# A transformer step on one core: the first feed-forward product of 20 of 22 gate/up pairs in seven block products instead of eight

## The chip, the cores and the metric

The kernel runs on one core of a Trainium2 chip. The metric is device microseconds (us) of one execution. Five engines matter here: PE (TensorE, the matrix unit), DVE (VectorE), ACT (ScalarE), POOL (GpSimd), and SP, which here only issues transfers. Each engine takes its instructions from a queue of its own in a fixed order; an instruction that waits for another engine holds everything behind it in that queue.

## What is computed

One layer of a hybrid network on 640 tokens (128 context, 512 latent) of width 1024, all float32: a token-mixing part, then a feed-forward part (2816 hidden channels). The change touches the feed-forward part:

```python
x = x + gt1 * rms_norm(y, norm_gains[1])
h = rms_norm(x, norm_gains[2]) * (1 + sc2) + sh2
gate, up = jnp.split(h @ w_ffn_in, 2, axis=-1)
y = (jax.nn.silu(gate) * up) @ w_ffn_out
x = x + gt2 * rms_norm(y, norm_gains[3])
```

## The kernel before

Float32 accuracy on PE comes from splits: an operand is kept as a high part (a cast to fp32r) and a low part (the rest), and every product is three matmuls, high by high, high by low, low by high (`mm3`, L81; its matmuls are lines L83, L84, L85). A split of a weight tile is done in halves of 512 columns: ACT casts the high part (L57), DVE subtracts for the low part (L58). Weight tiles come by SP transfers of 512 KB (`wr`), and their split parts `wh`, `wl` live in two pools of two slots each. The pools give a slot out again when the last reader of the tile in it is done.

The order in which each engine takes its instructions is set when the program is built. Around the output projection and the first feed-forward pairs PE's order is written out by hand (the loop under `manual_schedule`); elsewhere a scheduler places instructions by priority and by when it expects their inputs. `high()` raises the priority.

The end of the program goes through these stages:

- merge of two branches, into `mh`, `ml` (high and low part of the merged activations, 8 tiles of 128 channels by 640 tokens); beside it the sums for a gate row `gt1` (matmuls L208, L209 of `cph`, `cpl`, multiplied by `grow` in L225);
- output projection `acc<-woh,mh`, norm and modulation, token tile by token tile. `modulate` writes the next sub-layer's input back into `mh`, `ml` (L1083, L1084);
- first feed-forward product, `ffn(j, s)`: pair j is the gate tile and the up tile (128 hidden channels each), 8 tiles of k, three matmuls each, for a slice of the tokens. ACT takes silu of the gate (L1100), DVE multiplies by up (L1101), ACT and DVE split the result into `ah[j]`, `al[j]` (L1102, L1103). Pairs 0 and 1 run in slices of 384 and 256 tokens, in the hand-written order; pairs 2 to 21 in two halves of 320 tokens, so 2 x 2 x 8 x 3 = 96 matmuls of 320 columns per pair;
- second feed-forward product, `part`: two passes of 512 output channels, each with 11 steps `kk` of two k tiles, for five token tiles: 30 matmuls of 512 columns per step. In the first pass a generator (`row_job`) also sums the rows of a modulation block on DVE (L196);
- last norm, residual, output.

SBUF space is a stack of pools: a new pool lies where a closed one lay, and its tiles wait for the last users of the tiles that they cover. `fp0` holds `ah`, `al` of pairs 0 to 2; on it lies `bp2`, which holds the split weights of the output projection (`woh`, `wol`) and the norm's tiles.

## Time and profile before

| what | value |
|---|---|
| median of three runs | 1106.92 us (1103.74 to 1113.27) |
| profiled execution, span from first to last instruction | 1107.7 us |
| PE busy | 1054.9 us, 95% |
| DVE, ACT, POOL busy | 700.2, 416.4, 139.3 us |

The profiled execution has no time of its own besides its span; the span lies 0.8 us above the median. A busy PE counts overlapping matmuls: a matmul of 320 columns is listed with 0.31 us, but the next one starts 0.147 us after it, so PE's real price is read from starts and not from durations.

### The profile page before, as it was taken

What the parts mean: (1) busy time and instruction counts of PE and PEld (TensorE: products, weight loads), DVE (VectorE), ACT (ScalarE), POOL (GpSimd) and SP (SyncE); (2) the same over time, 40 slices, a digit from 0 to 9 for tenths busy, and PEclk for the clock granted to TensorE, in tenths of its full rate; (3) what the DMA queues carried; (4) which work ended last, traced back from release to release, by engine and by line L of the source; (5) the groups of instructions that cost most, each with busy time, mean ns of one, the idle gap of its engine ahead of it and who ended that gap; (6) DMA issues with size and microseconds to landing.
All of it is one profiled execution on the core that took longest, in us unless ns stands there. A gap on an engine that the chain in (4) does not pass through costs nothing.

```text
span 1107.7 us, 19821 instructions
## 1 busy us (share of the span) xinstructions
PE 1054.9 (95%) x7993; PEld 964.1 (87%) x7993; DVE 700.2 (63%) x1470; ACT 416.4 (38%) x809; POOL 139.3 (13%) x168
## 2 busy tenths in 40 slices
PE   6999988989889989999999999999999999999997
PEld 2699888779788888899998899999999999888885
DVE  5868996997888887986986853333333333464226
ACT  5668436428415333434235552222222222123110
POOL 2225411242242230101000000000000000000000
PEclk9999989998979999999999999999999999999998
DMA  9335621182164266548825412222222222452214
GB/s 345 135 90 155 177 70 64 58 190 83 53 147 124 75 140 235 170 146 304 302 94 179 168 44 91 76 77 76 77 76 77 77 77 77 152 190 76 95 39 152
DMA packets 46822, 139.43 MB, mean 126 GB/s; under 512 B 9453, under 2 KB 9970, under 8 KB 46730
## 3 DMA queue, kind: packets, MB, share of 16 engines
q1 hardware_dynamic: 42170, 125.01, 33.2%
q0 software_dynamic: 4560, 13.15, 5.4%
q8 instruction: 63, 1.03, 0.4%
q14 instruction: 29, 0.24, 0.1%
HBM read 115.47 MB, written 12.18 MB: 115 GB/s over the span
## 4 chain that ended last, share of the span: by engine, by line
PE 74%; DVE 11%; DMA 1%; ACT 1%; issue 1%; SPq 0%; DVEq 0%; POOL 0%; ACTq 0%
PE d L84 16%; PE d L85 16%; PE d L83 16%; PE acc L84 6%; PE acc L85 6%; PE acc L83 6%; DVE otmp L556 2%; PE s L640 2%; DVE X L558 2%; DVE wl L58 2%; PE v L611 1%; PE v L670 1%; DVE RT L562 1%; DMA AQ<-ea 1%; PE w L528 1%
## 5 line engine op out<-in xcount | busy, mean ns | idle before, releaser
L57 ACT CAST wh<-wr 128x512 fp32r<-128x512 f32 x238 | 138.1, 618 | 282.5 <-PE d L84 166.6
L58 DVE TENSOR_TENSOR wl<-wr,wh 128x512 fp32r<-128x512 f32 x238 | 162.0, 711 | 122.3 <-ACT wh L57 121.8
L84 PE MATMUL d<-hT,wh 128*128 128x320 f32 x720 | 230.0, 320 | 0.0
L83 PE MATMUL d<-hT,wh 128*128 128x320 f32 x720 | 228.5, 318 | 1.2 <-DVE cy L721 1.2
L85 PE MATMUL d<-hT,wl 128*128 128x320 f32 x720 | 228.9, 318 | 0.4 <-DVE wl L58 0.4
L83 PE MATMUL d<-mh,wh 128*128 128x320 f32 (+2 forms) x704 | 217.2, 309 | 0.0
L84 PE MATMUL d<-ml,wh 128*128 128x320 f32 (+2 forms) x704 | 217.1, 308 | 0.0
L85 PE MATMUL d<-mh,wl 128*128 128x320 f32 (+2 forms) x704 | 217.1, 308 | 0.0
L83 PEld LDWEIGHTS d<-hT,wh 128*128 128x128 f32 x720 | 138.2, 192 | 4.0 <-DVE cy L721 1.7
L85 PEld LDWEIGHTS d<-hT,wl 128*128 128x128 f32 x720 | 138.4, 192 | 3.3 <-issue 0.7
L84 PEld LDWEIGHTS d<-hT,wh 128*128 128x128 f32 x720 | 138.4, 192 | 2.9 <-issue 0.3
L83 PEld LDWEIGHTS d<-mh,wh 128*128 128x128 f32 x704 | 132.0, 187 | 0.1
L84 PEld LDWEIGHTS d<-ml,wh 128*128 128x128 f32 x704 | 132.0, 188 | 0.0
L85 PEld LDWEIGHTS d<-mh,wl 128*128 128x128 f32 x704 | 132.0, 187 | 0.0
L1101 DVE TENSOR_TENSOR zf<-zf,d 128x320 f32<-128x320 f32 x40 | 19.6, 489 | 131.7 <-PE d L85 131.7
L196 DVE SCALAR_TENSOR_TENSOR gacc<-wr,cv,gacc 128x1024 f32<-128x1024 f32 x64 | 80.1, 1278 | 18.1 <-DMA wr<-in_w_mod_dram 13.7
L83 PE MATMUL acc<-wh,ah 128*128 128x512 f32 x220 | 85.6, 389 | 0.0
L84 PE MATMUL acc<-wl,ah 128*128 128x512 f32 x220 | 85.6, 389 | 0.0
L85 PE MATMUL acc<-wh,al 128*128 128x512 f32 x220 | 85.6, 389 | 0.0
L190 POOL MEMSET gacc<- 128x1024 f32 x8 | 7.5, 963 | 365.5 <-PE d L85 305.7
L85 PEld LDWEIGHTS acc<-wh,al 128*128 128x128 f32 x220 | 41.3, 188 | 8.7
L83 PEld LDWEIGHTS acc<-wh,ah 128*128 128x128 f32 x220 | 41.3, 188 | 8.5
(302 smaller groups left out, 1581.0 us busy)
## 6 DMA issues: line engine op xcount, KB each, us to landing
wr<-in_w_in_dram SPq DMA_DIRECT2D x45, 512.0 KB, 3.3
wr<-in_w_ffn_in_dram SPq DMA_DIRECT2D x44, 512.0 KB, 3.3
wr<-in_w_mod_dram SPq DMA_DIRECT2D x32, 512.0 KB, 3.7
wr<-in_w_ffn_out_dram SPq DMA_DIRECT2D x22, 512.0 KB, 3.2
mr<-in_w_mod_dram SPq DMA_DIRECT2D x16, 512.0 KB, 8.4
thd<-gt SPq DMA_DIRECT2D x16, 320.0 KB, 3.0
bth<-thd SPq DMA_DIRECT2D x16, 320.0 KB, 4.0
wr<-in_w_br_dram SPq DMA_DIRECT2D x8, 512.0 KB, 6.8
```

What stands on the lines that cost most here:

```text
L57: (high or nc.scalar.copy)(out=hi[:, s], in_=raw[:, s])
L58: (low or nc.vector).tensor_tensor(out=lo[:, s], in0=raw[:, s], in1=hi[:, s].bitcast(F32), op=ALU.subtract)
L83: mm(out, lhsT=ah, rhs=bh, start=start, stop=False)
L84: mm(out, lhsT=ah, rhs=bl, start=False, stop=False)
L85: mm(out, lhsT=al, rhs=bh, start=False, stop=stop)
L196: nc.vector.scalar_tensor_tensor(out=acc[v], in0=w, scalar=self.cv[:, k, v:v + 1], in1=acc[v], op0=ALU.mult, op1=ALU.add)
L528: mm(pw[c2 * 64:c2 * 64 + 64, t * P:(t + 1) * P], lhsT=kq3[hs, 0, n, :], rhs=kq3[hs, :, n, :], start=True, stop=True)
L556: nc.vector.tensor_tensor(out=t, in0=B[:, j + 1:32, j:j + 1].broadcast_to([P, n, j]), in1=X[:, j:j + 1, 0:j].broadcast_to([P, n, j]), op=A ...
L558: nc.vector.tensor_tensor(out=X[:, j + 1:32, 0:j], in0=X[:, j + 1:32, 0:j], in1=t, op=ALU.subtract)
L562: nc.vector.transpose(out=RT.rearrange("p m x -> p x m"), in_=X)
L640: mm(ps[half(c2), o:o + 64], lhsT=w(d, c2, t, hd), rhs=R[:, d, c2, t, hd, :], start=True, stop=True)
L1101: nc.vector.tensor_tensor(out=a, in0=a, in1=pu, op=ALU.mult)
```

## The change

- Pairs 2 to 21 (`K1`, `K2` are the two halves of the eight k tiles, `ta`, `tb` the two halves of the tokens). Gate and up weights are a 2 x 2 block matrix, gate K1 (A11), gate K2 (A12), up K1, up K2 (A22); the activations are B11, B12 (K1 of ta, tb), B21, B22. Seven block products of 4 k tiles by three matmuls of 320 columns (`block`) take the place of eight. For that `prepare(j)` forms S1 to S4 of the raw weights (four additions or subtractions of 512 columns on DVE) and splits seven blocks; `combos` forms T1 to T4 of the activations once (DVE and ACT instructions of 1280 columns); T3 is written over B12, in `mh`, `ml`.
- A pair's products run in `first` (2 blocks), `second` (3) and `third` (2). PE's order is written out: first(j), third(j-1), second(j). Accumulators A and C are copied out by ACT in the middle (`p1`, `u2`, `u3`) and accumulated on.
- The result is kept whole, as `act[j]`. The split into high and low part is done later, in `split_act`, beside the second product; 12 split tiles of each kind fit, so pass 2 goes through the steps backwards, uses the last six steps' splits again and makes ten tiles' splits a second time.
- `fp0` holds two tiles (`act0`, `act1`) instead of six.
- Comments and docstrings are emptied, which moves line numbers.

The core of the diff:

```diff
-        ah = [fp0.tile([P, TOK], F32R, name=f"ah{j}") for j in range(3)]
-        al = [fp0.tile([P, TOK], F32R, name=f"al{j}") for j in range(3)]
+        act = [fp0.tile([P, TOK], F32, name=f"act{j}") for j in range(2)]
...
                 return
             pg, pu = half_done[j], self.gemm_cm(wf_in[j][1], h2, s)
-            a = fa()[:, 0:s.stop - s.start]
-            nc.scalar.activation(out=a, in_=pg, func=AF.Silu)
-            nc.vector.tensor_tensor(out=a, in0=a, in1=pu, op=ALU.mult)
-            nc.scalar.copy(out=ah[j][:, s], in_=a)
-            nc.vector.tensor_tensor(out=al[j][:, s], in0=a, in1=ah[j][:, s].bitcast(F32), op=ALU.subtract)
+            nc.scalar.activation(out=act[j][:, s], in_=pg, func=AF.Silu)
+            nc.vector.tensor_tensor(out=act[j][:, s], in0=act[j][:, s], in1=pu, op=ALU.mult)
...
-        # feed-forward network
-        fz, turn = zp.tile([P, 4, TOK], F32, name="zf"), itertools.cycle(range(4))
-        fa = lambda: fz[:, next(turn)]
         fst, fp = stack("fp")
+        txst, tx = stack("tx", side="right")
+        wgst, wg = stack("wg")
         past, psa = stack("psa2", 5, space=PSUM)
-        for j in range(3, FT):
-            ah.append(fp.tile([P, TOK], F32R, name=f"ah{j}"))
-            al.append(fp.tile([P, TOK], F32R, name=f"al{j}"))
         for j in range(2, FT):
-            for h in range(2):
-                ffn(j, slice(h * HALF, (h + 1) * HALF))
+            act.append(fp.tile([P, TOK], F32, name=f"act{j}"))
+        ta, tb = slice(0, HALF), slice(HALF, TOK)
+        K1, K2 = slice(0, 4), slice(4, 8)
+        B12, B22 = (mh[:, K1, tb], ml[:, K1, tb]), (mh[:, K2, tb], ml[:, K2, tb])
+        B11, B21 = (mh[:, K1, ta], ml[:, K1, ta]), (mh[:, K2, ta], ml[:, K2, ta])
+        T1, T2, T4 = ([tx.tile([P, 4, HALF], F32R, name=f"T{n}{x}") for x in "hl"] for n in (1, 2, 4))
+        T3 = B12
+        prepared, weights = {}, itertools.cycle((self.wpool, wf))
+        def load_j(j):
+            pl = (self.rpool, wg)[j % 2]
...
+        def prepare(j):
+            g, u = load_j(j)
+            slots = []
+            for _ in range(4):
+                pl = next(weights)
+                slots.append([pl.tile([P, KT, P], F32R, name="w" + x, tag="w" + x) for x in "hl"])
+            part = lambda x, n: [t[:, 4 * n:4 * n + 4] for t in slots[x]]
+            S = [wg.tile([P, 4, P], F32, name="S", tag="S", bufs=4) for _ in range(4)]
+            def halves(dst, src):
+                nc.scalar.copy(out=dst[0], in_=src)
+                nc.vector.tensor_tensor(out=dst[1], in0=src, in1=dst[0].bitcast(F32), op=ALU.subtract)
+                return dst
+            tt = lambda o, a, b, op: nc.vector.tensor_tensor(out=o, in0=a, in1=b, op=op)
+            o = {}
+            o["A11"] = halves(part(0, 0), g[:, K1])
+            tt(S[0], u[:, K1], u[:, K2], ALU.add)
+            o["S1"] = halves(part(0, 1), S[0])
+            tt(S[1], S[0], g[:, K1], ALU.subtract)
+            o["S2"] = halves(part(1, 0), S[1])
+            o["A12"] = halves(part(1, 1), g[:, K2])
+            tt(S[2], g[:, K1], u[:, K1], ALU.subtract)
+            o["S3"] = halves(part(2, 0), S[2])
+            o["A22"] = halves(part(3, 0), u[:, K2])
+            tt(S[3], g[:, K2], S[1], ALU.subtract)
+            o["S4"] = halves(part(3, 1), S[3])
+            prepared[j] = o
+        def combos():
+            tt = lambda o, a, b, op: nc.vector.tensor_tensor(out=o, in0=a, in1=b, op=op)
+            zz = zp.tile([P, 2, 4, HALF], F32, name="zf")
+            t1, t2, t3 = zz[:, 0], zz[:, 1], wg.tile([P, 4, HALF], F32, name="t3")
...
+            whole(t1, B11)
+            whole(t2, B12)
+            tt(t1, t2, t1, ALU.subtract)
+            halves(T1, t1)
+            whole(t3, B22)
+            tt(t1, t3, t1, ALU.subtract)
+            halves(T2, t1)
+            tt(t2, t3, t2, ALU.subtract)
+            halves(T3, t2)
+            whole(t3, B21)
+            tt(t3, t3, t1, ALU.subtract)
+            halves(T4, t3)
+        def block(ps, A, B, start, stop):
+            for k in range(4):
+                for n, (x, y) in enumerate(((0, 0), (0, 1), (1, 0))):
+                    nc.tensor.matmul(ps, lhsT=A[x][:, k], rhs=B[y][:, k], start=start and k == 0 and n == 0,
+                                     stop=stop and k == 3 and n == 2, skip_group_check=True)
+        acc = lambda: psa.tile([P, 512], F32, name="acc", tag="acc")[:, 0:HALF]
+        tmp = lambda n: wg.tile([P, HALF], F32, name=n, tag=n)
+        add = lambda o, a, b: nc.vector.tensor_tensor(out=o, in0=a, in1=b, op=ALU.add)
+        def first(j):
+            o = prepared[j]
+            A, C = acc(), acc()
+            block(A, o["A11"], B11, True, True)
+            p1 = tmp("p1")
+            with high():
+                nc.scalar.copy(out=p1, in_=A)
+            block(C, o["S1"], T1, True, True)
+            return dict(o=o, A=A, C=C, p1=p1)
+        def second(j, v):
+            o, A, C = v["o"], v["A"], v["C"]
+            block(A, o["S2"], T2, False, True)
+            u2, u3 = tmp("u2"), tmp("u3")
+            with high():
+                nc.scalar.copy(out=u2, in_=A)
+            B = fd()[:, 0:HALF]
+            block(B, o["A12"], B21, True, True)
+            with high():
+                add(act[j][:, ta], v["p1"], B)
+                nc.scalar.activation(out=act[j][:, ta], in_=act[j][:, ta], func=AF.Silu)
+            block(A, o["S3"], T3, False, True)
+            with high():
+                nc.scalar.copy(out=u3, in_=A)
+                add(act[j][:, tb], u3, C)
+            v["u2"] = u2
+        def third(j, v):
+            o, A, C = v["o"], v["A"], v["C"]
+            block(A, o["A22"], T4, False, True)
+            with high():
+                nc.vector.tensor_tensor(out=act[j][:, ta], in0=act[j][:, ta], in1=A, op=ALU.mult)
+            block(C, o["S4"], B22, False, True)
+            with high():
+                g = tmp("gb")
+                add(g, v["u2"], C)
+                nc.scalar.activation(out=g, in_=g, func=AF.Silu)
+                nc.vector.tensor_tensor(out=act[j][:, tb], in0=act[j][:, tb], in1=g, op=ALU.mult)
+        prepare(2)
+        with high():
+            combos()
+        with tc.manual_schedule(engines={mybir.EngineType.PE}):
+            last = None
+            for j in range(2, FT):
+                if j + 1 < FT:
+                    prepare(j + 1)
+                v = first(j)
+                if last:
+                    third(j - 1, last)
+                second(j, v)
+                last = v
+            third(FT - 1, last)
+        wgst.close()
+        txst.close()
         mst.close()
...
             return self.split(raw, [P, 2, 512], "w", next(pools))
-        def part(acc, w, kk, t):
...
+        def split_act(kk):
+            for k in (2 * kk, 2 * kk + 1):
+                hi, lo = (sp.tile([P, TOK], F32R, name="a" + x, tag="a" + x, bufs=12) for x in "hl")
+                nc.scalar.copy(out=hi, in_=act[k])
+                nc.vector.tensor_tensor(out=lo, in0=act[k], in1=hi.bitcast(F32), op=ALU.subtract)
+                parts_of[k] = hi, lo
+        def part(acc, w, kk, t, order):
             s = slice(t * P, (t + 1) * P)
             for i in range(2):
                 k = 2 * kk + i
-                self.mm3(acc, ah[k][:, s], al[k][:, s], w[0][:, i], w[1][:, i], k == 0, k == FT - 1)
+                self.mm3(acc, parts_of[k][0][:, s], parts_of[k][1][:, s], w[0][:, i], w[1][:, i],
+                         kk == order[0] and i == 0, kk == order[-1] and i == 1)
         TAIL = 4
         NK = FT // 2
         acc = [psa.tile([P, 512], F32, name="acc", tag="acc") for _ in range(NT)]
-        for kk in range(NK):
+        order = list(range(NK))
+        for kk in order:
+            split_act(kk)
             w = load_f(I["w_ffn_out"][0, kk])
             for t in range(NT):
-                part(acc[t], w, kk, t)
+                part(acc[t], w, kk, t, order)
             if kk >= 2:
                 next(fill, None)
...
             nc.vector.tensor_tensor(out=y0[:, t, :], in0=gt2[:, min(t, 1), 0:512], in1=acc[t], op=ALU.mult)
         acc = [psa.tile([P, 512], F32, name="acc", tag="acc") for _ in range(NT)]
-        for kk in range(NK - TAIL):
+        order = order[::-1]
+        for kk in order[:-TAIL]:
+            if kk < NK - 6:
+                split_act(kk)
             w = load_f(I["w_ffn_out"][1, kk])
             for t in range(NT):
-                part(acc[t], w, kk, t)
-        ws = [load_f(I["w_ffn_out"][1, kk]) for kk in range(NK - TAIL, NK)]
+                part(acc[t], w, kk, t, order)
+        ws = []
+        for kk in order[-TAIL:]:
+            split_act(kk)
+            ws.append(load_f(I["w_ffn_out"][1, kk]))
         for t in range(NT):
-            for i, w in enumerate(ws):
-                part(acc[t], w, NK - TAIL + i, t)
+            for kk, w in zip(order[-TAIL:], ws):
+                part(acc[t], w, kk, t, order)
             with tc.high_priority(offset=100000):
                 xx = fq.tile([P, D], F32, name="fx", tag="fx", bufs=2)
```

Three places where the order of instructions changes. DVE at the end of the merge (`wol` is the low part of the output projection's weights; the number behind a name is a buffer's). Before:

```order
L225 TENSOR_TENSOR gt1_5970<-grow_5973,d_6598 128x512 [waits PE_49]
L988 TENSOR_TENSOR bth_6530<-bth_6528,bth_6530 128x640 [waits DVE_49]
L58 TENSOR_TENSOR wol_6648<-wr_6645,woh_6647 128x512 [waits Activation_49]
L58 TENSOR_TENSOR wol_6656<-wr_6653,woh_6655 128x512 [waits Activation_49]
L990 TENSOR_TENSOR ml_5976<-bth_6530,mh_5975 128x640 [waits Activation_49]
L58 TENSOR_TENSOR wol_6648<-wr_6645,woh_6647 128x512
L58 TENSOR_TENSOR wol_6656<-wr_6653,woh_6655 128x512
L225 TENSOR_TENSOR gt1_5970<-grow_5973,d_6602 128x512 [waits PE_49]
L58 TENSOR_TENSOR cpl_6607<-gacc_5972,cph_6606 128x512 [waits Activation_49] x2
L225 TENSOR_TENSOR gt1_5970<-grow_5973,d_6612 128x512 [waits PE_49]
L225 TENSOR_TENSOR gt1_5970<-grow_5973,d_6616 128x512 [waits PE_49]
L58 TENSOR_TENSOR wol_6664<-wr_6661,woh_6663 128x512 [waits DMAHW2_49,Activation_49]
```

and with the change:

```order
L225 TENSOR_TENSOR gt1_5970<-grow_5973,d_6598 128x512 [waits PE_49]
L988 TENSOR_TENSOR bth_6530<-bth_6528,bth_6530 128x640 [waits DVE_49]
L225 TENSOR_TENSOR gt1_5970<-grow_5973,d_6602 128x512 [waits PE_49]
L58 TENSOR_TENSOR cpl_6607<-gacc_5972,cph_6606 128x512 [waits Activation_49]
L990 TENSOR_TENSOR ml_5976<-bth_6530,mh_5975 128x640 [waits Activation_49]
L58 TENSOR_TENSOR cpl_6607<-gacc_5972,cph_6606 128x512
L225 TENSOR_TENSOR gt1_5970<-grow_5973,d_6612 128x512 [waits PE_49]
L225 TENSOR_TENSOR gt1_5970<-grow_5973,d_6616 128x512 [waits PE_49]
L58 TENSOR_TENSOR wol_6644<-wr_6641,woh_6643 128x512 [waits Activation_49]
L58 TENSOR_TENSOR wol_6652<-wr_6649,woh_6651 128x512 [waits Activation_49]
L58 TENSOR_TENSOR wol_6644<-wr_6641,woh_6643 128x512 [waits Activation_49]
L58 TENSOR_TENSOR wol_6652<-wr_6649,woh_6651 128x512 [waits Activation_49]
```

The first four subtractions for `wol` stood on both sides of the last merged tile (`ml`); now they stand behind all of the gate row's work (`cpl`, `gt1`).

DVE at the start of pair 2, from the end of `modulate` of the last token tile on. Before:

```order
L1083 CAST mh_5975<-hf_7351 128x4x128 [waits Activation_49]
L1084 TENSOR_TENSOR ml_5976<-hf_7351,mh_5975 128x4x128 [waits DVE_49]
L1101 TENSOR_TENSOR fa_7399<-fa_7399,d_7374 128x384 [waits PE_49]
L1103 TENSOR_TENSOR al1_6636<-fa_7399,ah1_6633 128x384 [waits Activation_49]
L58 TENSOR_TENSOR wl_7566<-wr_7563,wh_7565 128x512 [waits DMAHW4_49,PE_49,Activation_49]
L58 TENSOR_TENSOR wl_7566<-wr_7563,wh_7565 128x512 [waits Activation_49]
L1101 TENSOR_TENSOR fa_7454<-fa_7454,d_7429 128x256 [waits PE_49,Activation_49]
L58 TENSOR_TENSOR wl_7574<-wr_7571,wh_7573 128x512 [waits DMAHW6_49,Activation_49]
L58 TENSOR_TENSOR wl_7574<-wr_7571,wh_7573 128x512 [waits Activation_49]
```

and with the change:

```order
L1099 TENSOR_TENSOR act1_6633<-act1_6633,d_7367 128x384 [waits PE_49]
L1166 TENSOR_TENSOR t3_7575<-mh_5975,ml_5976 128x1280 [waits DVE_49]
L1166 TENSOR_TENSOR T1l_7535<-zf_7574,T1h_7534 128x1280 [waits Activation_49]
L1166 TENSOR_TENSOR zf_7574<-t3_7575,zf_7574 128x1280 [waits DVE_49] x2
L1099 TENSOR_TENSOR act0_6632<-act0_6632,d_7419 128x256 [waits PE_49,Activation_49]
L1166 TENSOR_TENSOR t3_7575<-mh_5975,ml_5976 128x1280 [waits DVE_49]
L1166 TENSOR_TENSOR T2l_7537<-zf_7574,T2h_7536 128x1280 [waits Activation_49]
L1166 TENSOR_TENSOR t3_7575<-t3_7575,zf_7574 128x1280 [waits DVE_49]
L1166 TENSOR_TENSOR ml_5976<-zf_7574,mh_5975 128x4x320 [waits Activation_49]
L1166 TENSOR_TENSOR T4l_7539<-t3_7575,T4h_7538 128x1280 [waits Activation_49]
L1099 TENSOR_TENSOR act1_6633<-act1_6633,d_7471 128x256 [waits PE_49]
L1147 TENSOR_TENSOR wl_7545<-wr_7540,wh_7544 128x512 [waits DMAHW4_49]
```

`T1l`, `T2l`, `T4l` and the row that writes `ml` (T3) are new; the low part of A11 of pair 2 (`wl_7545`), which the third matmul of its first block reads, stands last.

ACT in the pairs' steady stretch, one cycle. Before (pairs 2 and 3; `zf` is silu of the gate):

```order
L1102 CAST ah2_6634<-zf_7518 128x320 [waits DVE_49]
L57 CAST wh_7813<-wr_7811 128x512 [waits DMAHW3_49,PE_49,Activation_49]
L57 CAST wh_7813<-wr_7811 128x512
L1100 ACTIVATE zf_7518<-d_7633 128x320 [waits PE_49]
L57 CAST wh_7821<-wr_7819 128x512 [waits DMAHW4_49,PE_49,Activation_49]
L57 CAST wh_7821<-wr_7819 128x512
L1102 CAST ah2_6634<-zf_7518 128x320 [waits DVE_49]
L1100 ACTIVATE zf_7518<-d_7703 128x320 [waits PE_49]
L1102 CAST ah3_7525<-zf_7518 128x320 [waits DVE_49]
L57 CAST wh_7937<-wr_7935 128x512 [waits DMAHW5_49,PE_49,Activation_49]
L57 CAST wh_7937<-wr_7935 128x512
L1100 ACTIVATE zf_7518<-d_7757 128x320 [waits PE_49]
```

and with the change (from the end of pair 2 to the middle of pair 4; `gb` is silu of gate for the tokens tb):

```order
L1235 ACTIVATE gb_7787<-gb_7787 128x320 [waits DVE_49]
L1214 COPY u2_7803<-acc_7734 128x320 [waits PE_49,Activation_49]
L1146 CAST wh_7706<-S_7713 128x512 [waits PE_49,Activation_49]
L1146 CAST wh_7706<-wr_7700 128x512
L1219 ACTIVATE act3_7515<-act3_7515 128x320 [waits DVE_49]
L1146 CAST wh_7708<-S_7714 128x512 [waits PE_49,Activation_49]
L1222 COPY u3_7804<-acc_7734 128x320 [waits PE_49,Activation_49]
L1205 COPY p1_7883<-acc_7869 128x320 [waits PE_49,Activation_49]
L1146 CAST wh_7839<-wr_7835 128x512 [waits DMAHW5_49,PE_49,Activation_49]
L1146 CAST wh_7839<-S_7847 128x512 [waits DVE_49]
L1146 CAST wh_7710<-wr_7702 128x512 [waits DMAHW4_49,PE_49,Activation_49]
L1146 CAST wh_7710<-S_7715 128x512
```

Seven casts of weights instead of four per pair, and three copies out of accumulators (`p1`, `u2`, `u3`) with two silu between them; the silu `gb` of the pair before stands ahead of `u2`.

## Rows read from the trace of the kernel before

**Rows 1.** The page: PE's total; granted clock in 40 slices, tenths.
```profile
PE 1054.9 (95%) x7993; PEld 964.1 (87%) x7993; DVE 700.2 (63%) x1470; ACT 416.4 (38%) x809; POOL 139.3 (13%) x168
...
PEclk9999989998979999999999999999999999999998
```

**Rows 2.** Busy time by stage: stretch and length, then each engine, clock, DMA.
```profile
637.00:666.50 29.50, 29.50 (x210) 29.42 (x209) 16.94 (x42) 15.12 (x34) 0.53 (x1) 1.00 0.15 54
...
807.00:948.00 141.00, 141.00 (x963) 141.00 (x963) 44.21 (x80) 38.90 (x80) 0.00 (x0) 1.00 0.22 76
948.00:1023.00 75.00, 75.00 (x332) 61.82 (x331) 39.90 (x49) 16.38 (x31) 1.84 (x2) 1.00 0.43 151
```

**Rows 3.** PE by time: start, duration; end of pair 1, first and last matmul of pairs 2 to 21.
```profile
666.24 0.28 PE L84 MATMUL d<-ml,wh 128*128 128x256 f32 x1
666.35 0.28 PE L85 MATMUL d<-mh,wl 128*128 128x256 f32 x1
666.46 0.30 PE L83 MATMUL d<-mh,wh 128*128 128x320 f32 x1
...
947.91 0.31 PE L85 MATMUL d<-mh,wl 128*128 128x320 f32 x1
948.06 0.40 PE L83 MATMUL acc<-wh,ah 128*128 128x512 f32 x1
```

**Rows 4.** Groups by line and shape from 620 us on: busy, mean ns | idle before.
```profile
L58 DVE TENSOR_TENSOR wl<-wr,wh 128x512 fp32r<-128x512 f32 x124 | 80.1, 688 | 102.8 <-ACT wh L57 102.7
L57 ACT CAST wh<-wr 128x512 fp32r<-128x512 f32 x124 | 70.8, 619 | 176.3 <-PE d L84 84.6 <-PE acc L85 39.6 <-DMA wr<-in_w_ffn_out_dram 36.7
...
L196 DVE SCALAR_TENSOR_TENSOR gacc<-wr,cv,gacc 128x1024 f32<-128x1024 f32 x16 | 19.8, 1281 | 13.2 <-DMA wr<-in_w_mod_dram 9.1 <-DMA gacc<-in_b_mod_dram 4.2
L1101 DVE TENSOR_TENSOR zf<-zf,d 128x320 f32<-128x320 f32 x40 | 19.6, 489 | 131.7 <-PE d L85 131.7
...
L1100 ACT ACTIVATE zf<-d 128x320 f32<-128x320 f32 x40 | 17.4, 434 | 43.0 <-PE d L85 43.0
```

**Rows 5.** The end of the merge by time: ACT, then DVE, then PE.
```profile
576.76 0.72 ACT L989 CAST mh<-bth 128x640 fp32r<-128x640 f32 x1 [0.25 <-DVE bth L988]
...
576.65 1.28 DVE L58 TENSOR_TENSOR wol<-wr,woh 128x512 fp32r<-128x512 f32 x2
...
575.57 0.40 PE L83 MATMUL acc<-woh,mh 128*128 128x512 f32 x1
577.39 0.50 PE L84 MATMUL acc<-wol,mh 128*128 128x512 f32 x1 [1.42 <-DVE wol L58]
```

**Rows 6.** DVE by time, from the last `modulate` to the end of pair 1.
```profile
654.07 0.43 DVE L1083 CAST mh<-hf 128x512 fp32r<-128x512 f32 x1 [0.24 <-ACT hf L1081]
654.53 0.69 DVE L1084 TENSOR_TENSOR ml<-hf,mh 128x512 fp32r<-128x512 f32 x1
...
667.21 1.29 DVE L58 TENSOR_TENSOR wl<-wr,wh 128x512 fp32r<-128x512 f32 x2
```

**Rows 7.** Stretches around waits of PE earlier in the program; columns as in Rows 2.
```profile
317.20:320.30 3.10, 0.02 (x1) 0.00 (x0) 3.10 (x5) 0.00 (x0) 2.13 (x2) 1.00 0.99 239
320.30:327.10 6.80, 5.76 (x23) 5.79 (x24) 5.27 (x11) 0.00 (x0) 0.00 (x0) 0.51 0.25 53
235.90:237.20 1.30, 0.12 (x2) 0.00 (x1) 1.30 (x4) 0.44 (x1) 0.00 (x0) 1.00 0.45 95
```

**Rows 8.** DVE by time where pair 21 ends, PE having started its last matmul at 947.91.
```profile
948.33 0.49 DVE L1101 TENSOR_TENSOR zf<-zf,d 128x320 f32<-128x320 f32 x1 [1.75 <-PE d L85]
949.35 0.49 DVE L1103 TENSOR_TENSOR al<-zf,ah 128x320 fp32r<-128x320 f32 x1 [0.53 <-ACT ah L1102]
```

**Rows 9.** Groups by line and shape, 500 to 637 us: instructions of 640 columns.
```profile
L990 DVE TENSOR_TENSOR ml<-bth,mh 128x640 fp32r<-128x640 f32 x8 | 6.5, 818 | 0.4 <-ACT mh L989 0.4
...
L989 ACT CAST mh<-bth 128x640 fp32r<-128x640 f32 x8 | 5.8, 727 | 13.1 <-DVE bth L988 13.1
```

**Rows 10.** The page's transfers: KB each, us from issue to landing.
```profile
wr<-in_w_ffn_in_dram SPq DMA_DIRECT2D x44, 512.0 KB, 3.3
```

More of the change, by code (lines that the diff above doesn't have):

```diff
@@ L1087, in run @@
         half_done = {}
-        fa = lambda: bp.tile([P, 384], F32, name="fa", tag="fa", bufs=2)
         def ffn(j, s, part=None):
@@ new lines, in run @@
+        ta, tb = slice(0, HALF), slice(HALF, TOK)
[7 more added lines that the diff above has]
+            pl = (self.rpool, wg)[j % 2]
+            raw = []
+            for i in range(2):
+                r = pl.tile([P, KT, P], F32, name="wr", tag="wr", bufs=2)
+                nc.sync.dma_start(out=r, in_=I["w_ffn_in"][2 * j + i])
+                raw.append(r)
+            return raw
@@ new lines, in combos, with whole, halves @@
+        def combos():
+            tt = lambda o, a, b, op: nc.vector.tensor_tensor(out=o, in0=a, in1=b, op=op)
+            zz = zp.tile([P, 2, 4, HALF], F32, name="zf")
+            t1, t2, t3 = zz[:, 0], zz[:, 1], wg.tile([P, 4, HALF], F32, name="t3")
+            def whole(o, b):
+                tt(o, b[0].bitcast(F32), b[1].bitcast(F32), ALU.add)
+            def halves(dst, src):
+                nc.scalar.copy(out=dst[0], in_=src)
+                tt(dst[1], src, dst[0].bitcast(F32), ALU.subtract)
+            whole(t1, B11)
[10 more added lines that the diff above has]
+            halves(T4, t3)
@@ L1138, in load_f @@
             return self.split(raw, [P, 2, 512], "w", next(pools))
-        def part(acc, w, kk, t):
+        spst, sp = stack("sp")
+        parts_of = {}
+        def split_act(kk):
[5 more added lines that the diff above has]
+        def part(acc, w, kk, t, order):
             s = slice(t * P, (t + 1) * P)
@@ L1182, in run @@
                 nc.sync.dma_start(out=dst[:, 512:1024], in_=xx[:, 512:1024])
-        for st in (fq_st, past, fst, f0st, wst2, wst):
+        for st in (fq_st, spst, past, fst, f0st, wst2, wst):
             st.close()
```

## The prediction

> **What bounds the kernel now.** I read the page first: PE is busy 95% of the span [rows 1]. Then the stages: from 637 us to the end of the second product PE is busy without a gap at full clock, while DVE uses 44 of 141 us and ACT 39 of 141 in the first product [rows 2]. So in the stage that the change rewrites only PE's work counts, and DVE and ACT have two thirds of their time free. Last, PE's instructions by time, for the price of a matmul: pairs 2 to 21 start at 666.46, their last matmul at 947.91, and the second product follows 0.15 us later without a wait [rows 3]. These are 20 x 96 = 1920 matmuls in 281.6 us, 0.1467 us each. The listed 0.31 us is a duration that overlaps with the next matmul; whoever multiplies by it counts the gain twice.
>
> **Matmuls removed.** 84 instead of 96 per pair, so 240 fewer in all, and the order of PE's instructions shows 240 fewer rows. Each kept its shape, 128x128 by 320 columns. 240 x 0.1467 = 35.2 us less on PE. A block of twelve takes 1.76 us, a pair 12.3 us where it took 14.1. All of this is on the path, if the other engines keep up.
>
> **Do they keep up?** DVE per pair: 11 instructions of 512 columns (four sums, seven low parts; 0.69 us, or 0.64 when two stand back to back [rows 4, 6]) and five of 320 columns (0.49 [rows 4]), 9.5 to 10 us of 12.3. ACT: seven casts at 0.62 and five instructions of 320 columns at 0.43 [rows 4], 6.5 us. Neither is full, but both queues are in order, so I followed one cycle through them. PE's seven blocks run first, first, third, third, second, second, second. The weight slots return after blocks 2, 6, 7 and, for the last, block 4 of the next cycle, and each is filled within 3 us and read five blocks (8.8 us) after its return: safe. The raw weights' transfers take 3.3 us [rows 10]; the one for `up` can start only when A22 of the pair before is split, and lands some 0.7 us before DVE comes to it. If it is late, DVE waits, but DVE has 2 us free per cycle, and nothing that PE needs within 4 us stands behind it. The tightest place is the copy `u2`. PE's third block of `second` accumulates on the same accumulator, 3.5 us after the end of block 4. On ACT `u2` stands behind the casts A22 and S4 (released by that end, 1.2 us) and behind silu of `gb`, which waits for DVE's add (0.2 us until the end is seen, 0.49 for the add). Casts and silu are done 0.2 + 1.2 + 0.43 = 1.8 us after block 4; block 5, which `u2` also waits for, ends at 1.76 + 0.2; the copy ends at 2.4. That leaves 1.1 us. So I take no wait in the steady stretch, with 0 and 1.2 us per pair as the ends (1.2 being this slack lost once again).
>
> **Start of the output projection.** With `fp0` ten kilobytes smaller, `woh` lies over tiles of the gate row, and its casts and subtractions come behind them. Before, DVE's first two `wol` began at 576.65 and PE, which had waited 1.42 us for them, went on at 577.39 [rows 5]. Now five instructions of 512 columns (`gt1`, `cpl`, `cpl`, `gt1`, `gt1`) and the `ml` of 640 (0.82 [rows 9]) come first: 5 x 0.62 + 0.74 = 3.8 us. The four matmuls of the gate row that PE did afterwards are now done before (0.23 us each, as 512 columns start [rows 3], 0.9 us). Cost: 2.9 us. The later weights of this stage move by as much as PE does.
>
> **Start of pair 2.** T3 overwrites B12, which pair 1 reads until its last matmul. So after that matmul: T3's cast on ACT and then, on DVE, T3's low part, T4's low part, pair 1's product and at last the low part of A11, for which the third matmul of pair 2 waits. No row has 1280 columns. From 512 and 640 columns on ACT (0.619 and 0.727 [rows 4, 9]) I get 1.26 us, on DVE from 512 and 1024 columns (0.688, 1.281 [rows 4]) and 512 and 640 (0.688, 0.818 [rows 9]) 1.47 to 1.58, I take 1.49. The chain is 0.2 + 1.26 + 1.49 + 1.49 + 0.42 + 0.69 = 5.55, less 0.15 for overlapping starts and 0.3 for the two matmuls that go ahead: 5.1 us. Before this, two of the sums come between the halves of the last `modulate`: the last `ml` began at 654.53 [rows 6] and now ends near 657.6. The 96 matmuls of 256 columns of pairs 0 and 1 start 0.113 us apart and end at 666.46 [rows 3], so they begin at 655.6 and need that tile from the 14th on, at 657.0: 0.7 us. The rest of the sums (some 15 us on DVE) lies beside these 96 matmuls. Sum: 5.8 us; the bounds are 0 (T3's chain hidden, which only another order could do) and 7.
>
> **End of pair 21.** The second product now needs `act0` split, and ACT does that behind the last silu: end of PE seen 0.2, add 0.49, silu 0.43, cast of 640 columns 0.73, first matmul at 1.9. DVE's part of it stands behind two subtractions (1.3) and pair 21's product (0.49): 0.2 + 0.49 + 1.3 + 0.49 + 0.82 = 3.3, so the third matmul starts at 3.4 to 3.5. Less two matmuls, 3.0 us. Before, PE went straight on while DVE and ACT finished pair 21 behind it [rows 3, 8]. In the last cycle `third` follows `second` at once and waits for the copy `u3`: 0.6 us. Sum 3.6.
>
> **Second product.** 32 splits are added (0.82 us on DVE, 0.73 on ACT [rows 9]), 26 and 23 us, where DVE is busy 40 of 75 us in the first pass [rows 2]; 44 splits of 320 columns each have gone from the first product. In the first pass DVE then has 40 + 22 x 0.8 = 58 of 75 us. The split tiles are made up to six steps ahead (a step is 30 x 0.23 = 6.8 us of PE), which covers DVE's waits for the row sums' transfers. In pass 2 the ten repeated splits reuse tiles freed four steps earlier. I take 0.
>
> **The clock.** A wait costs more than its length if PE's clock falls. [...] Bounds 0 and 8 in all.
>
> **Sum.** -35.2 + 2.9 + 5.8 + 3.6 + 0 + 8.0 = -14.9 us. Against the profiled span of 1107.7 that is 1092.8; the span lies 0.8 above the median shown, so 1092.0.
>
> **Rivals.**
> *Cheap starts* (0.20): the clock stays up in two of the three places or the chains overlap better. For it: the waits are broken up by single matmuls. -35.2 + 12.3 + 2.4 gives 1087; with no fall 1084.
> *ACT's order costs each pair a wait* (0.17): `u2` late by the slack of 1.1 us and more, because `gb`'s add on DVE comes late. For it: DVE is busy 80% of a pair with instructions that wait in order. Against: 1.1 us of room, and DVE free when block 4 ends. 0.5 to 1.2 us per pair, 10 to 24 us: 1102 to 1116, no change.
> *DVE sets the pace, slower than before* (0.08): the added sums and splits cost more than their listed time, so that PE waits for low parts in every pair. It is slower by 1% from 1118 - 1092 = 26 us, 1.3 us per pair, a DVE cycle of 13.6 us, 0.85 us for each of its 16 instructions. Against it, two subtractions in 1.29 us [rows 6], less than twice 0.69. [...]
> That the products are not fewer is excluded by the order.
>
> **How the numbers follow.** A measurement of this kernel tells about 1% (11 us) from no change. Forecast 0.55, within it some four fifths below 1095.9. Faster: 0.44 + 0.20 = 0.64. Same: 0.11 + 0.16 = 0.27. Slower: 0.09. The range is 1081 (cheap starts, with half of pair 2's wait gone too) to 1108 (a pair loses 0.8 us); it leaves out the slower rival, the upper third of the one before and a little below.
>
> **What would show it.** In the changed kernel's profile: blocks of twelve matmuls 1.76 us long, pairs 12.3 us apart; waits of PE before the first `wol` (some 5 us in pieces), before pair 2's third matmul (5 us, released by DVE) and before the second product (3 us, in two pieces), each with a clock of 0.5 behind it; no wait of PE inside pairs 3 to 20. I am wrong if such waits recur (then on `u2` or a low part), if DVE's cycle is over 12.3 us, or if the second product shows waits past its first step.

## The result, and the profile after

| | median us | runs |
|---|---|---|
| before | 1108.76 | 4 (1103.74 to 1113.27) |
| changed | 1093.89 | 4 (1093.29 to 1095.66) |

The ratio is 0.9866, 95% interval 0.9834 to 0.9898: 14.9 us less, where 14.9 was forecast. That the totals agree says little of the terms, which follow.

The changed kernel's page, PE's total and the granted clock in 40 slices, against [rows 1]: 240 matmuls fewer, and three new slices below 9, which begin at 573, 655 and 928 us (a slice is 27.3 us).

```profile
PE 1027.7 (94%) x7753; PEld 933.3 (86%) x7753; DVE 830.7 (76%) x1670; ACT 482.2 (44%) x921; POOL 139.5 (13%) x168
...
PEclk9999989998989999999998998999999999899999
```

To find where the time went I divided both traces at the starts of the same five matmuls: the gate row's first, pair 0's first, pair 2's first, the second product's first and its last. Lengths in us:

| profiled run | up to gate row | to pair 0 | pairs 0, 1 | pairs 2 to 21 | second product | rest | span |
|---|---|---|---|---|---|---|---|
| before | 574.65 | 62.33 | 29.48 | 281.60 | 151.47 | 8.17 | 1107.7 |
| changed | 571.26 | 67.65 | 30.33 | 259.39 | 154.39 | 8.58 | 1091.6 |
| difference | -3.39 | +5.32 | +0.85 | -22.21 | +2.92 | +0.41 | -16.1 |
| forecast | 0 | +5.3 | +0.7 | -24.1 | +3.2 | 0 | -14.9 |

(The forecast of -24.1 is -35.2 for matmuls, 5.1 + 2.4 at pair 2, 3.6 at the end of pair 21.) The first column is not the change: five kernels below whose code up to there is the same as the changed kernel's need 569.3 to 576.9 us for it. That is the noise of this kernel; from the gate row on the change gives -12.7 us.

Busy time of the changed kernel by stage, columns as in [rows 2]. In the first and last rows PE stands and the clock falls; in the two rows between, 19 pairs long, PE never stands, and DVE is at 72 to 75%.

```profile
669.00:684.00 15.00, 10.62 (x59) 10.36 (x58) 14.78 (x22) 7.31 (x13) 0.00 (x0) 0.77 0.22 71
684.00:800.00 116.00, 116.00 (x793) 116.00 (x792) 86.50 (x153) 56.54 (x115) 0.00 (x0) 1.00 0.28 87
800.00:918.00 118.00, 118.00 (x807) 118.00 (x806) 84.40 (x150) 56.97 (x115) 0.00 (x0) 1.00 0.26 81
918.00:930.00 12.00, 6.15 (x34) 5.41 (x33) 6.68 (x12) 5.69 (x12) 1.84 (x2) 0.91 0.68 222
```

All waits of PE from 560 to 1100 us in the changed kernel: who waits for whom, us in total, how often, the longest.

```profile
PE acc L83 <- ACT ah L1275: 4.4, 1, 4.4
PE acc L1192 <- DVE wl L1147: 4.4, 1, 4.4
PE d L209 <- DVE cpl L58: 1.6, 2, 0.8
PE acc L1192 <- ACT u L1222: 1.4, 1, 1.4
PE d L84 <- DVE ml L1083: 0.5, 1, 0.5
PE d L208 <- ACT cph L57: 0.5, 1, 0.5
PE acc L84 <- DVE wol L58: 0.4, 1, 0.4
PE acc L83 <- ACT woh L57: 0.2, 1, 0.2
```

**Start of the output projection**, PE by time and DVE's `wol`, against [rows 5]: the gate row's matmuls now stand ahead of the first `woh`, each behind its own wait, and the first `wol` comes behind them.

```profile
571.26 0.39 PE L208 MATMUL d<-cph,onesr 128*128 128x512 f32 x1
...
575.93 0.51 PE L209 MATMUL d<-cpl,onesr 128*128 128x512 f32 x1 [0.84 <-DVE cpl L58]
576.63 0.79 PE L83 MATMUL acc<-woh,mh 128*128 128x512 f32 x1 [0.19 <-ACT woh L57]
577.83 0.80 PE L84 MATMUL acc<-wol,mh 128*128 128x512 f32 x1 [0.40 <-DVE wol L58]
...
577.09 2.49 DVE L58 TENSOR_TENSOR wol<-wr,woh 128x512 fp32r<-128x512 f32 x4
```

From the gate row's first matmul to the first `wol` product are 6.57 us; before they were 2.74 with four matmuls less (0.92). That is 2.9 us. The other 2.4 of the 5.3 are the clock's: from the first `wol` product on twelve matmuls start 0.44 us apart on average, which at full clock start 0.23 us apart.

**Start of pair 2**, PE, then DVE, then ACT by time, and last a stretch of DVE alone (length, DVE's busy time, clock, DMA). DVE has no gap from 655.8 us to the end of the `wl` (A11's low part) that PE waits for. ACT's cast of T3 (`mh<-zf`) waits 0.26 us for pair 1's last reading of that tile and begins at 668.08, while pair 1 still runs to 669.24. It ends at 669.35, and DVE comes to T3's low part (`ml<-zf,mh`) only at 670.18.

```profile
669.13 0.28 PE L85 MATMUL d<-mh,wl 128*128 128x256 f32 x1
...
669.38 0.31 PE L1192 MATMUL acc<-ml,wh 128*128 128x320 f32 x1
674.07 0.63 PE L1192 MATMUL acc<-mh,wl 128*128 128x320 f32 x1 [4.38 <-DVE wl L1147]
...
668.78 1.49 DVE L1166 TENSOR_TENSOR t<-t,zf 128x1280 f32<-128x1280 f32 x1
670.18 1.49 DVE L1166 TENSOR_TENSOR ml<-zf,mh 128x1280 fp32r<-128x1280 f32 x1
671.59 1.49 DVE L1166 TENSOR_TENSOR T4l<-t,T4h 128x1280 fp32r<-128x1280 f32 x1
673.00 0.41 DVE L1099 TENSOR_TENSOR act<-act,d 128x256 f32<-128x256 f32 x1
673.33 0.69 DVE L1147 TENSOR_TENSOR wl<-wr,wh 128x512 fp32r<-128x512 f32 x1
...
668.08 1.27 ACT L1174 CAST mh<-zf 128x1280 fp32r<-128x1280 f32 x1 [0.26 <-PE d L85]
...
655.82:674.00 18.18, 18.18 (x18) 0.94 0.00 0
```

**End of pair 21**, ACT and PE by time, against [rows 3, 8]. The copy `u` (`u3`) stands behind two casts of the second product's weights. The last silu and the casts to `ah` stand behind two more, whose transfer landed only at 926.4.

```profile
918.93 1.14 ACT L57 CAST wh<-wr 128x512 fp32r<-128x512 f32 x2 [0.24 <-ACT act L1219]
919.97 0.42 ACT L1222 COPY u<-acc 128x320 f32<-128x320 f32 x1
926.46 1.14 ACT L57 CAST wh<-wr 128x512 fp32r<-128x512 f32 x2 [6.07 <-DMA wr<-in_w_ffn_out_dram]
927.50 0.47 ACT L1235 ACTIVATE gb<-gb 128x320 f32<-128x320 f32 x1
927.87 2.59 ACT L1275 CAST ah<-act 128x640 fp32r<-128x640 f32 x4
...
923.92 0.31 PE L1192 MATMUL acc<-mh,wl 128*128 128x320 f32 x1
928.63 0.79 PE L83 MATMUL acc<-wh,ah 128*128 128x512 f32 x1 [4.41 <-ACT ah L1275]
```

**The clock** behind the three waits, columns as in [rows 7]: half speed (0.50) in all three stretches of 6.6, 4.7 (from the end of pair 2's wait on) and 6.8 us.

```profile
576.40:583.00 6.60, 6.01 (x14) 4.44 (x14) 3.17 (x6) 2.17 (x5) 0.00 (x0) 0.50 0.43 151
...
674.00:678.70 4.70, 4.63 (x17) 4.63 (x18) 4.70 (x9) 2.70 (x5) 0.00 (x0) 0.50 0.01 3
...
927.90:934.70 6.80, 6.07 (x14) 4.79 (x15) 6.80 (x10) 6.80 (x12) 0.00 (x0) 0.50 0.48 183
```

### The profile page after: what moved, and what is told of

The parts are those of the page before. It is cut to its first block, busy times and chain, and to the rows that moved or that the text cites. A ratio compares the mean times of both kernels' runs of the same rounds, so it can differ in the third digit from the quotient of the medians.

```text
span 1091.6 us, 19746 instructions
## 1 busy us (share of the span) xinstructions
PE 1027.7 (94%) x7753; PEld 933.3 (86%) x7753; DVE 830.7 (76%) x1670; ACT 482.2 (44%) x921; POOL 139.5 (13%) x168
## 4 chain that ended last, share of the span: by engine, by line
PE 70%; DVE 13%; DMA 2%; ACT 1%; issue 1%; SPq 1%; DVEq 0%; POOL 0%; ACTq 0%
PE acc L1192 19%; PE d L84 7%; PE d L85 7%; PE d L83 7%; PE acc L84 6%; PE acc L83 6%; PE acc L85 6%; PE d L1192 3%; PE s L640 2%; DVE X L558 2%; DVE otmp L556 2%; DVE wl L58 2%; PE v L611 1%; PE v L670 1%; DMA ea<-scr 1%
## 5 line engine op out<-in xcount | busy, mean ns | idle before, releaser
L57 ACT CAST wh<-wr 128x512 fp32r<-128x512 f32 x158 | 92.3, 617 | 145.6 <-PE d L84 84.2
L58 DVE TENSOR_TENSOR wl<-wr,wh 128x512 fp32r<-128x512 f32 x158 | 109.3, 716 | 42.7 <-ACT wh L57 42.4
L1192 PE MATMUL acc<-mh,wl 128*128 128x320 f32 x240 | 75.2, 313 | 4.4 <-DVE wl L1147 4.4
L1192 PE MATMUL acc<-ml,wh 128*128 128x320 f32 x240 | 74.9, 312 | 0.0
L1192 PE MATMUL acc<-mh,wh 128*128 128x320 f32 x240 | 74.9, 312 | 0.0
L1146 ACT CAST wh<-wr 128x512 fp32r<-128x512 f32 x60 | 37.1, 619 | 69.2 <-issue 44.3
L1146 ACT CAST wh<-S 128x512 fp32r<-128x512 f32 x80 | 49.5, 620 | 30.0 <-PE d L1192 21.4
L1147 DVE TENSOR_TENSOR wl<-wr,wh 128x512 fp32r<-128x512 f32 x60 | 41.5, 691 | 21.1 <-ACT wh L1146 20.0
L1147 DVE TENSOR_TENSOR wl<-S,wh 128x512 fp32r<-128x512 f32 x80 | 54.9, 687 | 1.9 <-ACT wh L1146 0.6
L1192 PEld LDWEIGHTS acc<-mh,wl 128*128 128x128 f32 x240 | 45.6, 190 | 4.6 <-DVE wl L1147 4.6
```

Of the source, the lines that this page charges most:

```text
L57: (high or nc.scalar.copy)(out=hi[:, s], in_=raw[:, s])
L58: (low or nc.vector).tensor_tensor(out=lo[:, s], in0=raw[:, s], in1=hi[:, s].bitcast(F32), op=ALU.subtract)
L1146: nc.scalar.copy(out=dst[0], in_=src)
L1147: nc.vector.tensor_tensor(out=dst[1], in0=src, in1=dst[0].bitcast(F32), op=ALU.subtract)
L1192: nc.tensor.matmul(ps, lhsT=A[x][:, k], rhs=B[y][:, k], start=start and k == 0 and n == 0, stop=stop and k == 3 and n == 2, skip_group_che ...
```

## The experiments

Open were: what each of the three starts costs and by which mechanism; whether PE sets the pace of a pair or DVE; and whether the clock's fall has a price of its own. Each edit is made to the changed kernel, each time below is of one run unless an interval stands with it, and stages are those of the table above.

### One start at a time

`e1_room`: six tiles in `fp0` again, so that `woh` lies over the same room as before.

```diff
-        act = [fp0.tile([P, TOK], F32, name=f"act{j}") for j in range(2)]
+        act = [fp0.tile([P, TOK], F32, name=f"act{j}") for j in range(6)]
...
-        for j in range(2, FT):
+        for j in range(6, FT):
```

> Six act tiles are kept in fp0 instead of two, which fills the 15 kB that ah and al of three pairs took; nothing else changes. Theory (woh lies over tiles of the gate row, so its casts queue behind that row's work and PE's clock falls): from the gate row's first matmul to pair 0's first matmul the stretch goes back from 67.7 us to that of the kernel before, 62.3 us, with the clock at full speed in it; the rest stays. Rival (the stretch is longer because the merge ended at another moment, or because of transfers): it stays at 67 us.

1088.51 us; gate row to pair 0 takes 62.86 us instead of 67.65 (before: 62.33), PE's wait there is the one of before, 1.4 us for `wol`, and the clock stays at 1.00 from 574 to 586 us. So all but 0.5 us of this cost is where the tiles lie. The rest of the kernel didn't quite stay the same: pairs 0 and 1 take 30.92 us instead of 30.33, with waits for `mh` and `ml` (why, this run doesn't show).

`e2_order`: pair 2's weights are prepared ahead of the sums, and T4 is formed last.

```diff
-        prepare(2)
         with high():
-            combos()
+            prepare(2)
+            rest = combos()
+        rest()
```

(`rest` is the last three lines of `combos`: `whole(t3, B21)`, the subtraction, `halves(T4, t3)`.)

> prepare(2) gets the raised priority and stands ahead of combos, and the three steps that lead to T4 come after it at normal priority. Theory (DVE's in-order queue of combos, busy without a gap from the last modulate on, holds the low part of A11): PE's wait of 4.5 us at pair 2's third matmul falls under 1.5 us, the clock does not fall there, and from pair 2's first matmul to the second product's first the stretch goes from 259.4 to about 253 us. Rival, as the prediction had it (T3 has to wait for pair 1's last reading of B12 and holds what is behind it): T3 still waits, and PE's wait moves to the block that reads T3 or T2, 2 us or more.

1090.43 us; pairs 2 to 21 take 254.89 us, 4.50 less (about 253 were expected). From pair 2's first matmul to its `third` block are 84 matmuls, 12.32 us without a wait; the changed kernel takes 19.03, this one 15.45. What is left are three waits of 0.6 to 0.8 us for `wl` and T2's low part, with some slower matmuls around them, and the clock stays full:

```profile
672.00:684.00 12.00, 10.81 (x72) 10.16 (x71) 11.66 (x15) 7.33 (x11) 0.00 (x0) 1.00 0.29 89
```

T3 is still written over B12 here, and no matmul waits for T3. Together with the changed kernel's trace, where DVE had work without a gap and T3's cast was done before DVE came to it, this shows that the wait at pair 2 was the order of DVE's queue, not the tile that T3 shares. (The other 0.9 of the 4.50 us is a shorter wait before the second product, 3.5 us, see below.) T3 with a tile of its own wasn't tried.

`e3_end`: the row sums' transfers begin one step later, so that the transfer of step 3's weights is issued ahead of them.

```diff
-            if kk >= 2:
+            if kk >= 3:
+                next(fill, None)
+            if kk == 4:
                 next(fill, None)
```

> The row sums beside the second product start one step later (and do two steps at once at step 4), so that the weight transfer of step 3 is issued ahead of the first transfer for the row sums; ACT's order stays the same. Theory (ACT stands before pair 21's last silu in a cast that waits for this transfer, and the casts of act0 stand behind it): PE's wait before the second product's first matmul falls from 4.6 to about 2.5 us. Rival (the wait is the chain add, silu, cast, or the place of the split tiles): it stays above 4 us.

1093.32 us. The wait before the second product is 2.1 us instead of 4.4, pairs 2 to 21 take 256.51 us. The two casts still stand ahead of the silu, but no longer wait for a transfer:

```profile
928.03 1.14 ACT L57 CAST wh<-wr 128x512 fp32r<-128x512 f32 x2 [3.78 <-PE acc L1192]
929.08 0.47 ACT L1235 ACTIVATE gb<-gb 128x320 f32<-128x320 f32 x1
```

This wait varies from run to run: in the five runs that leave this place alone (`e1_room`, `e2_order`, `e5_eight`, `e7_dve3`, `e10_warm`) it is 3.5, 3.5, 3.2, 2.8 and 3.5 us. In the changed kernel the first of the two casts is released by the transfer's landing, and the second product starts 2.2 us after that cast's start (926.46, 928.63); `e6_all` below, with the same edit as here, has 2.1 us again. So the transfer's share is 2.3 us of the changed kernel's 4.4, and 0.7 to 1.4 us in the others, an estimate by the same subtraction. Of the 2.88 us that pairs 2 to 21 save here, 0.6 don't belong to the edit: at pair 2, behind the same wait of 4.4 us, matmuls ran at half clock for 3.3 us (0.267 us from start to start) instead of 4.7. The total shows nothing of the saving, since this run needed 576.85 us to the gate row, 5.6 more than the changed kernel's.

### Who sets the pace of a pair

`e5_eight`: block A12 by B21 is multiplied twice per pair, eight products instead of seven; DVE and ACT do what they did.

```diff
             block(B, o["A12"], B21, True, True)
+            block(B, o["A12"], B21, True, True)
```

> The block product A12 B21 is made twice in every pair, overwriting itself, so that a pair has eight blocks again with DVE's and ACT's work of seven; the result does not change. Theory (PE sets the pace in the steady stretch, 0.1467 us per matmul): plus 20 x 1.76 = 35.2 us, so about 1129 us, and 36 us over the kernel with the change shows what the waits at the joints cost. Rival (DVE or ACT sets the pace in part of the cycle): less than 30 us more.

1124.40 us; pairs 2 to 21 take 293.62 us, 34.2 more, although the wait before the second product is 1.2 us shorter (3.2): 35.4 for 240 matmuls, 35.2 by the price of one. A pair takes 14.08 us where the changed kernel takes 12.32, both 0.1467 us times the matmuls. The total is only 30.5 us over the changed kernel's median, where 35.2 was expected and under 30 was the rival's sign; in the profiled runs the stretch up to the gate row is 2.0 us shorter than the changed kernel's, and the second product 1.4, with less of it at half clock. So it is the pairs, and not the total, that speak against the rival.

`e7_dve3`: three subtractions of 512 columns more on DVE per pair, whose result is S4 as before.

```diff
+            for _ in range(3):
+                tt(S[3], g[:, K2], S[1], ALU.subtract)
             prepared[j] = o
```

> The changed kernel with three more subtractions of 512 columns on DVE in each pair's preparation (S4 computed four times over; the result is the same). DVE's cycle grows from 9.2 to about 9.2 + 3 x 0.65 = 11.2 us of 12.3. Theory (PE sets the pace, DVE has 3 us free per pair): pairs 2 to 21 within 1.5 us of 259.4 us, no wait of PE in pairs 3 to 20 over 0.3 us. Rival (DVE's order already sets the pace, or an instruction costs more than listed): 1 to 2 us per pair more, 280 to 300 us.

1093.97 us; a pair takes 12.32 us as before, with DVE at 88 to 90%:

```profile
688.00:804.00 116.00, 116.00 (x793) 116.00 (x793) 104.54 (x181) 57.37 (x113) 0.00 (x0) 1.00 0.28 87
804.00:922.00 118.00, 118.00 (x806) 118.00 (x806) 103.98 (x181) 57.69 (x114) 0.00 (x0) 1.00 0.27 86
```

PE sets the pace, and DVE has room for three more instructions of this kind. (Pairs 2 to 21 take 259.19 us, nearly the changed kernel's 259.39, but by chance: 0.5 us less at pair 2, 1.6 less in the wait before the second product, 1.9 more at the end of pair 21, where PE waits 1.8 us for `u3` and the clock falls.)

### The clock's own price

`e10_warm`: 28 matmuls into an accumulator that nobody reads, ahead of pair 2's third matmul; PE works where it stood.

```diff
+            if j == 2:
+                idle = fd()[:, 0:HALF]
+                for i in range(28):
+                    nc.tensor.matmul(idle, lhsT=o["A11"][0][:, 0], rhs=B11[i % 2][:, 0], ...)
             block(A, o["A11"], B11, True, True)
```

> The changed kernel with 28 extra matmuls of 320 columns ahead of pair 2's third matmul, into an accumulator that nothing reads: PE works (28 x 0.147 = 4.1 us) where it waited 4.4 us. Theory (the clock falls because PE stands, and that costs 2.4 us over and above the wait): the clock stays full in pair 2, pairs 2 to 21 counted from pair 2's first matmul at 259.4 - 2.4 = 257.0. Rival (the low clock behind a wait costs nothing that counts, or falls for another reason): 259.4 or more.

1093.70 us; pairs 2 to 21 take 257.11 us with the clock at 1.00 from 664 to 690 us. That the expected 257.0 is met is in part luck: 0.9 of the 2.3 us saved is the shorter wait before the second product, 3.5 us here; only 1.4 us were saved at pair 2. There 12.32 us of matmuls have become 17.62, of which 28 x 0.1467 = 4.1 are the extra ones and about 1.0 two waits for `wl`. In the changed kernel they have become 19.03, of which 4.54 is the wait (4.69 between two starts, less 0.15). So the low clock cost 19.03 - 12.32 - 4.54 = 2.2 us, and it went as soon as PE was kept busy; the two waits for `wl`, which the changed kernel doesn't have, took part of it back.

### All together

`e6_all` makes the edits of `e1_room`, `e2_order` and `e3_end` together.

> The three edits of e1_room, e2_order and e3_end together. Theory (three separate waits with the clock's fall behind two of them, nothing shared): the single savings add up: gate row to pair 0 at 62.9 us (4.8 less than in the changed kernel), pairs 2 to 21 at 259.4 - 4.5 - 2.9 = 252.0, the rest as it was; 1093.9 - 12.2 = 1081.7 us. Rival (what is saved early is given back later by DVE's queue, which is fuller around pair 2): pairs 2 to 21 at 254 or more, total 1084 to 1088.

1080.92 us (4 runs, 1078.91 to 1087.55); ratio to before 0.9751, 95% interval 0.9711 to 0.9791. Gate row to pair 0 63.21 us, pairs 2 to 21 253.50 (252.0 expected, 254 by the rival), second product 151.71. The total is the expected one within the spread. The 1.5 us by which pairs 2 to 21 save less are two items that didn't belong into the sum: 0.9 of `e2_order`'s 4.5 was a shorter wait before the second product, which `e3_end` counts too, and 0.6 of `e3_end`'s 2.9 was the clock at pair 2. Without them it is 259.4 - 3.6 - 2.3 = 253.5. So the savings add up.

`e9_ahead` is `e6_all` with `act0` and `act1` split early, into the tile `zf` that held the sums of the activations; ten split tiles of each kind are left for the rest. The core of its edit against `e6_all`:

```diff
             third(FT - 1, last)
+        zh = zp.tile([P, 4, TOK], F32R, name="zf")
+        for k in range(2):
+            nc.scalar.copy(out=zh[:, 2 * k], in_=act[k])
+            nc.vector.tensor_tensor(out=zh[:, 2 * k + 1], in0=act[k], in1=zh[:, 2 * k].bitcast(F32), op=ALU.subtract)
...
-        parts_of = {}
+        parts_of = {k: (zh[:, 2 * k], zh[:, 2 * k + 1]) for k in range(2)}
```

> e6_all, and the first step's two activation tiles (act0, act1) are split before pair 21 ends, into the tile that held the sums of the activations. Theory (the wait before the second product is only the chain behind pair 21's end on ACT and DVE): that wait is gone, and with it the clock's fall; pairs 2 to 21 some 2.1 us less than in e6_all (about 250), second product 151.5 as in the kernel before; in all about 5 us less than e6_all, 1077 us. Rival (the weights' casts of this place are late by themselves): a wait of 1 us or more stays on wh or wl, 1080 us or more.

1080.07 us (6 runs, 1078.30 to 1085.06); ratio to before 0.9739, 95% interval 0.9714 to 0.9764. Both waits at the end are gone. With its operands ready early, the second product's first seven matmuls are placed ahead of pair 21's `third`, into the time in which `u3` was waited for:

```profile
913.02 0.30 PE L1195 MATMUL acc<-mh,wl 128*128 128x320 f32 x1
913.16 0.40 PE L83 MATMUL acc<-wh,zf 128*128 128x512 f32 x1
...
914.79 0.41 PE L1195 MATMUL acc<-T4h,wh 128*128 128x320 f32 x1
```

From the gate row to the last matmul's start the profiled runs take 524.88 (before), 511.76 (changed), 499.34 (`e6_all`) and 494.12 us (`e9_ahead`). So in the trace the early split gives 5.2 us, as expected, but the medians of the two differ by 0.85 us with ranges of 7 to 9 us: by them the two can't be told apart, and the 1077 us expected were not reached. The profiled run is the fastest of the six here, and the third of four of `e6_all`; the stretch ahead of the gate row, which varies by 7.6 us among the kernels with equal code there, could hide 5 us in so few runs, but what takes the difference back is not shown. `e9_ahead` beats both kernels: 2.6% under before, where the change as made gives 1.3%.

## Why the prediction was right, step by step

- **Matmuls removed, 35.2 us: right.** A pair takes 12.32 us in every kernel that has seven products, and 14.08 with eight (`e5_eight`).
- **No wait in the steady stretch: right**, and so both rivals that put one there fall. In a cycle of the changed kernel `u2` ends at 706.55 and the block that needs it starts at 707.63: 1.08 us of room, 1.1 forecast. DVE's cycle is 86.5 / 116 x 12.32 = 9.2 us (9.5 to 10 forecast), and 11.1 us in `e7_dve3` without a wait.
- **Start of the output projection, 2.9 + 2.4: right**, 5.3 us, and 4.8 of it undone by the room alone (`e1_room`).
- **Start of pair 2, 5.1 + 2.4 and 0.7 for `ml`: size nearly right, mechanism wrong.** It cost 4.5 + 2.2, and pairs 0 and 1 took 0.85 more. The step that failed is "T3 overwrites B12, which pair 1 reads until its last matmul. So after that matmul: T3's cast". B12 is the K1 half; pair 1's last matmuls read K2, so the cast began 1.2 us before pair 1's end (the shared tile held it up by 0.26 us), and DVE wasn't waiting for it: from 655.8 us on it had 1280-column sums back to back. The forecast also put "the rest of the sums (some 15 us on DVE)" beside pairs 0 and 1 without adding up what DVE had to do by their end; that sum is what was late. It met the size since nearly the same instructions stand last in the queue (two of 1.40 from start to start, 0.4, 0.6).
- **Bounds there, 0 and 7: held**, with 4.5 + 0.85 us without the clock. But the lower one was put down to T3's chain alone; `e2_order` leaves T3 where it was, and takes 3.6 of the 6.7 us at pair 2 away.
- **End of pair 21, 3.0 + 0.6: the term that was mis-sized**, 4.6 + 1.6 measured. The forecast counted DVE's two subtractions ahead of the last product, but on ACT, "behind the last silu", not the casts of the second product's weights that stand ahead of `u3` and ahead of that silu, nor the transfer that the last two wait for. The first matmul came 4.6 us after PE's end, not at 1.9; without the wait for the transfer (`e3_end`) at 2.3.
- **Second product, 0: right.** With the clock full it takes 151.7 us (`e6_all`), before 151.5; in the first 75 us of the changed kernel's second product DVE is busy 51, fewer than the 58 forecast.
- **The clock, 8.0: size right.** The 8.0 of the sum was the author's estimate, 2.4 for the output projection's start, 2.4 for pair 2 and 3.2 for the second product, and no run shows it. The runs showed 2.4 + 2.2 + 2.7 (154.39 - 151.71), 7.3 in all, with the clock at 0.50 in each of the three places. Behind pair 2's wait matmuls of 320 columns start 0.267 us apart instead of 0.147, 1.8 times; in the kernel before they do so too, in the stretch at 0.51 [rows 7]. And the price isn't fixed: behind the same wait at pair 2 it was 1.6 us in `e3_end` and `e7_dve3`, where matmuls ran at half clock for 3.3 and 3.4 us and not 4.7.
- **Sum.** From the gate row on -12.7 instead of -14.9, the 2.6 us of pair 21's end being most of the miss. The medians differ by 14.9 all the same; that the last two microseconds agree is luck, within the interval (1.0% to 1.7%). The time itself came out 1.9 us above the 1092.0 forecast; the median before rose by as much with its fourth run (1106.92 to 1108.76).

## What to carry to other kernels

When the matmuls of a long steady stretch get fewer, the saving there can be counted from starts (here it came out exactly) and the questions are its two ends: list everything that stands in each in-order queue up to the first instruction that PE needs, also work of the next stage and the transfer it waits for, and add it up from where the queue was last idle. Of the saved 35 us some 22 went again at three such places, each with waits and 2 to 3 us lost to the half clock behind them, and an order or a place in memory removed most of it. A total that agrees proves none of its terms: here the mechanism at pair 2 was wrong with the right size.

## What the runs showed of the hardware

- A wait's length alone doesn't tell whether the clock falls. Behind the 2.1 us wait before the second product it fell in `e3_end` (0.50 from 931.0 to 934.4 us) and stayed at 1.00 in `e6_all`. In `e7_dve3` it fell behind the 1.8 us wait for `u3` and not behind the 2.8 us wait that followed (the two rows below, columns as in [rows 2]). Behind the waits of 3.2 to 4.4 us before the second product it fell (changed kernel, `e1_room`, `e2_order`, `e5_eight`, `e10_warm`: matmuls of 512 columns start 0.43 us apart instead of 0.23), and behind the 4.4 us at pair 2 too (changed kernel, `e3_end`, `e5_eight`, `e7_dve3`: 0.267 us instead of 0.147 at 320 columns). What else decides is open.

```profile
924.50:927.80 3.30, 3.30 (x14) 3.30 (x13) 0.42 (x2) 0.00 (x0) 0.00 (x0) 0.50 0.69 237
928.00:936.00 8.00, 5.16 (x27) 4.01 (x26) 5.70 (x9) 5.86 (x11) 1.84 (x2) 1.00 0.71 251
```

- The wait before the second product, which in the changed kernel ends behind a transfer's landing, varied by 1.6 us among kernels with equal code there (2.8 in `e7_dve3`, 4.4 in the changed kernel).
- In the changed kernel a DVE instruction of 1280 columns takes 1.49 us and the next one starts 1.40 after it; a cast of 1280 on ACT takes 1.27. The forecast had scaled 1.49 and 1.26 from shorter rows.
